# Two edits to a planner's inputs in a hybrid encoder layer: where the embedding gate's last four row blocks are cast, and where the last feed-forward part's first two units begin

## Chip, cores and metric

The kernel runs on one core of one Trainium2 chip. The metric is device time in microseconds (us) of one execution. Before the change three timed runs gave 1155.58, 1153.28 and 1151.23 us, so a median of 1153.28 us. One more execution was profiled.

## What is computed

One encoder layer on 256 rows of width 2048, in float32. Cut to the matrix products, which are nearly all of the work:

```python
u = rms_norm(h, g_mix_pre) @ w_in                       # 2048 x 5120
mixed = concat(norm(attention), norm(recurrence)) @ w_out
h = h + rms_norm(mixed, g_mix_post)
fn = rms_norm(h, g_ffn_pre)
ff = (silu(fn @ w_ffn_gate) * (fn @ w_ffn_up)) @ w_ffn_down   # inner width 5632
h = h + rms_norm(ff, g_ffn_post)
gate = sigmoid(rms_norm(h, g_ple_pre) @ w_ple_gate)     # 2048 x 2048
h = h + rms_norm(gate * (p @ w_ple_proj), g_ple_post)
```

## The kernel before

**Products and weight tiles.** A product of two float32 matrices is made of three matmuls (`mm3`, lines 694 to 696, 705 to 707): each operand is split into a rounded part (`hi`, `wh`) and the rest (`lo`, `wl`), and hi*hi, lo*hi and hi*lo are summed in PSUM. A weight tile is 2 blocks of 128 rows by 512 columns, 512 KB. It goes through three engines: SyncE (SP) issues its load into a raw buffer `wr` (line 568, or 551 in the feed-forward stage), ScalarE (ACT) rounds it into `wh` (line 643, `hi_stream`), VectorE (DVE) subtracts to get `wl` (line 656, `lo_stream`), and TensorE (PE) then runs 12 matmuls of 128x512 on it (`products`): 2 blocks, 2 halves of the 256 rows, 3 matmuls each. The third matmul of each three reads `wl`, so it can start later than the first two. There are four pairs `wh`/`wl` (`W_BUFS`) and four buffers `wr` (`R_BUFS`): a cast must wait until PE is done with the tile four back, and a load until DVE is done with the tile four back. Some loads of the feed-forward stage use further buffers, named `third` and `lower` in the trace.

**The order of the work.** Each engine gets its instructions in one fixed order. That order comes from a planner (`Plan`, lines 93 to 212) that runs when the kernel is built: every helper is a generator that yields the engine and estimated cost of its next instruction, and the planner takes the one that could start first, by its estimated clocks plus a bias (`late`). `plan.add(gen, ready, late)` hands it a generator that is not to start before `ready`. The order of PE's main products is written out by hand (`segs`); everything else is fitted around it.

**The feed-forward stage** runs in three parts (`PARTS`) of 4, 4 and 3 column chunks of the inner width. Each part makes its chunks (gate and up products, line 1890 on, group kind "up"), moves them into transposed form and multiplies them by `w_ffn_down` (kind "down"). Most groups save products in the manner of Strassen's scheme: some pairs of row blocks are treated as a unit of 2x2 blocks that needs seven products instead of eight. Such a unit begins with `four_products` (line 718), four of the seven, which need two weight tiles of which one is a sum of weight blocks: DVE makes the sums at lines 591, 595 and 601 (`sum_stream`) from a tile in `wr` or `third` and one in `lower`. The table `FOURS` (line 522) tells at which pair of weight tiles of the group ahead each unit of the next group begins. The last part's first down group has two units; its entry, ("up3", "down2"), is (2, 4): the first unit begins ahead of the third pair of the last up group, the second ahead of the fifth and last pair.

**The embedding gate.** Its left operand is the normed residual stream, transposed: 16 row blocks of 128 (`hP`, in the trace `hT_ffn_hi` and `hT_ffn_lo`). `next_norm` makes the new `h` on DVE in four chunks of 512 columns. Three of them are transposed by PE (line 330). The last goes through `turn_h` (line 1590): DVE transposes 32x32 squares (line 1596), 16 DMAs of 32 KB move the squares into the tile `mT` (`moved`, line 349, 12 of them issued by POOL and 4 by SP), and then four times ACT makes a block of `hT_ffn_hi` (line 317) and DVE a block of `hT_ffn_lo` (line 319). These are row blocks 12 to 15. The gate's products run over eight pairs of row blocks and, in turns, over the first two column chunks: tiles 0 and 1 use blocks 0 and 1, and so on, so that tiles 12 and 13 use blocks 12 and 13 and tiles 14 and 15 use blocks 14 and 15. Below, "tile n" is the n-th weight tile of the embedding gate, counted from 0.

Of the kernel before, what the change touches and what calls it, by code (L numbers as in the profile page):

```python
# [72 lines left out]
LATE = 0.8  # L73
EARLY = 3
SOON = 2.0
ADDED = 6.0
AHEAD = 5
ISSUE = 160
# [148 lines left out]
def dve(n, take=None, give=None):  # L227
    return ("dve", COST["dve"] + 0.00104 * n, None, take, give)
# [11 lines left out]
def layer(ctx: ExitStack, tc: tile.TileContext, a: dict, out: bass.AP):  # L240
# [5 lines left out]
    plan = Plan(wr=R_BUFS, w=W_BUFS, sm=SM_BUFS, acc=4, ev=1, mid=2, bt=2, m2=1, mt=1, sq=1, T0=1, T1=1, T4=1, **{f"{s}{j}": n for s, m, n in (("p", 5, 1), ("t", 4, 0)) for j in range(m)}, wr0=1, w0=1)  # L246
# [52 lines left out]
    def col(name, i):  # L299
        c = VEC_COLS[name][0] + i  # L300
        return vec[:, c : c + 1]
# [13 lines left out]
    def gained_split(hi, lo, src, g, give=None):  # L315
        yield act(S)
        nc.scalar.activation(hi, src, AF.Copy, scale=g)  # L317
        yield dve(S, give=give)
        nc.vector.scalar_tensor_tensor(  # L319
            out=lo, in0=src, scalar=g, in1=f32(hi), op0=ALU.mult, op1=ALU.subtract  # L320
        )
# [11 lines left out]
    def moved(e, here, take, tile_of, turn=True, pool=()):  # L333


        if turn:
            flat = e.rearrange("p t n -> p (t n)")
            yield dve(2 * N)
            nc.vector.transpose(out=flat, in_=flat)
        src = e.rearrange("p t (k j b) -> p t k j b", j=4, b=32)  # L340
        mT = None
        for j in range(4):
            for i in range(4):
                first = None if mT else take
                yield ("pool" if i in pool else "dma", COST["move"], None, first, None)
                if mT is None:
                    mT = tile_of()
                dst = mT.rearrange("p t k (i b) -> p t k i b", b=32)
                (nc.gpsimd if i in pool else nc.sync).dma_start(  # L349
                    dst[32 * j : 32 * j + 32, :, :, i, :],  # L350
                    src[32 * i : 32 * i + 32, :, :, j, :],
                )
        done(here)
        return mT.rearrange("p t k q -> p k t q")
# [16 lines left out]
    def done(event):  # L371
        event.t = plan.now
# [63 lines left out]
    class Group:  # L436
# [84 lines left out]
    }  # L521
    FOURS = {
        ("up0", "up3"): (3, 5, 7), ("up3", "up3"): (2, 3, 4), ("up3", "down4"): (2, 3, 3, 4),
        ("down4", "down4"): (1, 2, 3, 3), ("down4", "up3"): (1, 2, 3), ("up3", "down2"): (2, 4),
    }
    fours = {}

# [82 lines left out]
    def added(dst, src, ev):  # L610
        yield ("pool", COST["move"], None, None, None)
        nc.gpsimd.dma_start(dst, src, accum_op=ALU.add)  # L612
        plan.now += ADDED
        done(ev)

    def last_sum(i):
        late, last, j, js, _, _ = fours[i]
        b = OUT[j]
        there = Event()
        yield from added(blocks()[:, b, :], late[:, 0, :], there)  # L620
        yield there
        if j == js[-1]:
            raws[last] = blocks()[:, slice(3, 7, 3) if not js[0] else slice(1, 8, 6) if js[1:] else slice(7, 8), :]
            done(ev_raw[last, 2])
# [21 lines left out]
    def lo_stream():  # L646
        last_one = max(f[1] for f in fours.values())
        for i in range(len(tiles)):
# [16 lines left out]
            if i in fours:  # L665
                plan.add(last_sum(i), plan.now, -2 * SOON)

# [50 lines left out]
    def four_products(group, j, i):  # L718
# [16 lines left out]
        if last:  # L735
            plan.add(made_of_four(group), plan.clk["pe"] + plan.SEM, -SOON)
            plan.run()

    def made_of_four(group):

        (C1, _, _), (C2, _, _) = group.chunks
        (q1, q7), (q5, q6) = C1.accs, C2.accs
        there = Event()

        def second():
            yield act(N)
            nc.scalar.copy(q7, v)
            done(there)

        yield ev_rf  # L750
        yield act(N)
        u, v = (t2["pool"].tile([P, N], F32, tag="junk", name="u", bufs=2) for _ in range(2))
        nc.scalar.copy(u, q1)
        yield dve(N)
        nc.vector.tensor_tensor(out=u, in0=u, in1=q6, op=ALU.subtract)
        yield dve(N)
        nc.vector.tensor_tensor(out=v, in0=u, in1=q7, op=ALU.subtract)
        plan.add(second(), plan.now, -SOON)
        yield dve(N)
        nc.vector.tensor_tensor(out=q6, in0=q5, in1=v, op=ALU.subtract)  # L760
        yield dve(N)
        nc.vector.tensor_tensor(out=q5, in0=q5, in1=u, op=ALU.subtract)
        yield there
        done(group.made)
# [768 lines left out]
    def next_norm(sub, nxt, rstd, ev_rstd, g_next):  # L1533
# [24 lines left out]
        for c in range(4):  # L1558
            if c > 1:
                yield nxt.ev[4 * c - 8]  # L1560
            for b in range(2):
                sl = slice(c * N + b * S, c * N + (b + 1) * S)
                for t in range(NT):
                    yield dve(S)
                    nc.vector.scalar_tensor_tensor(
                        out=h[:, t, sl], in0=mg[:, t, sl], scalar=ro[:, t : t + 1],
                        in1=h[:, t, sl], op0=ALU.mult, op1=ALU.add,
                    )
                if c < TURNED:
                    plan.add(transpose_h(4 * c + 2 * b, hi, lo, nxt, sub.gname), plan.now)  # L1570
            if c >= TURNED:
                plan.add(turn_h(c, hi, lo, nxt, sub.gname), plan.now, -SOON)
        yield nxt.ev[4 * TURNED - 3]
# [16 lines left out]
    def turn_h(c, hi, lo, nxt, gname):  # L1590

        for t in range(NT):
            yield dve(N, take=None if t else "mid")
            if not t:
                e = mid_tile()
            nc.vector.transpose(out=e[:, t, :], in_=t2["h"][:, t, c * N : (c + 1) * N])
        there = Event()
        mT = yield from moved(e, there, "mt", mT_tile, turn=False, pool=(0, 1, 2) if nxt is hP else ())
        plan.free["mid"].append(plan.now)
        yield there  # L1600
        for b in range(4):
            kk = 4 * c + b
            yield from gained_split(
                *(x[:, kk, :].rearrange("p (t q) -> p t q", t=NT) for x in (hi, lo)), mT[:, b],
                col(gname, kk), give="mt" if b == 3 else None,
            )
            done(nxt.ev[kk])
# [106 lines left out]
    hP = Act()  # L1714
# [3 lines left out]
    def gate_post(f):  # L1718
        def post(ch):
            yield ev_rf  # L1720
            for t in range(NT):
                yield act(N, SILU, take=None if t else "mid")
                if t == 0:
                    es[f] = mid_tile()
                nc.scalar.activation(
                    es[f][:, t, :], ch.accs[t], AF.Silu, scale=rstd_f[:, t : t + 1]
                )
            ch.release()
        return post

    def mid_tile():
        return t2["pool"].tile([P, NT, N], F32, tag="mid", name="mid", bufs=2)
# [4 lines left out]
    def up_post(f, mid, kk0, g, soon):  # L1737

        def post(ch):
            yield g.free  # L1740
            e = es.pop(f)
            for t in range(NT):
                yield dve(N)
                nc.vector.scalar_tensor_tensor(
                    out=e[:, t, :], in0=ch.accs[t], scalar=rstd_f[:, t : t + 1], in1=e[:, t, :],
                    op0=ALU.mult, op1=ALU.mult,
                )
            ch.release()
            there = Event()
            mT = yield from moved(e, there, "mt", mT_tile, pool=(0, 2) if soon else range(4))  # L1750
            plan.free["mid"].append(plan.now)
            yield there
            plan.add(carried(mid, kk0, mT), plan.now + (0.5 if soon else {0: 12.0, 9: 6.0}.get(f, 3.0)), -SOON if soon else 0.0)
        return post

    def carried(mid, kk0, mT):
        summed = any(kk0 <= kx < kk0 + 4 for kx in mid.ev_sums)
        for b in range(0, 4, 2):
            kk = kk0 + b
            i, j = divmod(kk, 8)  # L1760
            hi, lo = mid.tiles(i)
            yield from split(
                *(by_tile(x[:, j : j + 2, :]) for x in (hi, lo)), mT[:, b : b + 2], 2 * S,
                give="mt" if b and not summed else None,
            )
            mid.pair(kk)
        if summed:
            plan.add(mid_sums(mid, kk0, mT), plan.now + (20.0 if mid.name[-1] == str(2) else 0.0))
# [106 lines left out]
    for part, (f0, f1) in enumerate(PARTS):  # L1875
        mid = Mid(f"mid{part}")
        last_part = part == len(PARTS) - 1
        for f in range(f0, f1):
            slot = ring()
            g = Chunk(gate_post(f), slot=slot)  # L1880
            u = Chunk(up_post(f, mid, (f - f0) * 4, g, f == f1 - 1), late=(-3 if f == f1 - 1 else -1) * SOON, slot=slot)
            groups.append(Group(
# [331 lines left out]
```

## Time and profile before

| what | value |
|---|---|
| median of the three timed runs | 1153.28 us |
| the profiled execution, its own time | 1154.53 us |
| span of its trace, first to last instruction | 1152.7 us |
| TensorE busy | 1139.3 us (99%) |
| VectorE busy | 923.4 us (80%) |
| ScalarE busy | 722.0 us (63%) |
| mean granted TensorE clock | 0.996 |

The page of the profile gives busy times and the chain of work that ended last. A row of the timeline gives the start and the length of an instruction, and in square brackets how long its engine sat idle before it and what ended that. Matmuls overlap, so that the distance between two starts, not the length, tells how fast PE goes.

### The profile page before, as it was taken

The page shows a single profiled execution, that of the slowest core. Times are in us where ns is not written, and L with a number is a line of the kernel's source. Part 1 is how long each engine was busy: PE and PEld are TensorE (multiplying, and loading weights), DVE is VectorE, ACT ScalarE, POOL GpSimd, SP SyncE. Part 2 cuts the span into 40 slices and gives each one's busy share as a digit, 9 for nine tenths or more (in the row PEclk, how much of TensorE's full clock was granted, in tenths as well). Part 3 has the DMA queues.
Part 4 walks back from the last instruction along what each step waited for, and adds up shares of the span by engine and source line. Part 5 has one row for each costly group of instructions (what it writes and reads, how often), then busy time and mean ns, then how long its engine had stood idle before and what let it go on. Part 6 is the DMA issues. An engine that isn't in the chain of part 4 may idle for free.

```text
span 1152.7 us, 15162 instructions
## 1 busy us (share of the span) xinstructions
PE 1139.3 (99%) x5199; PEld 946.3 (82%) x5199; DVE 923.4 (80%) x1161; ACT 722.0 (63%) x954; POOL 145.7 (13%) x232
## 2 busy tenths in 40 slices
PE   9999999999999999999999999999999999999897
PEld 7888888888888888888888888888888888888786
DVE  6578786888468779998988898989988888769474
ACT  7777777876447645656566556666555655557473
POOL 0000000000000033142110223312111303101000
PEclk9999999999999999999999999999999999999999
DMA  9867665546685996787877786897887678866661
GB/s 323 287 188 224 186 180 191 178 150 207 226 287 176 316 291 210 239 243 218 282 259 221 248 239 213 252 273 238 259 303 247 200 246 271 287 237 213 200 216 73
DMA packets 110270, 267.97 MB, mean 232 GB/s; under 512 B 36272, under 2 KB 43184, under 8 KB 108784
## 3 DMA queue, kind: packets, MB, share of 16 engines
q1 hardware_dynamic: 96304, 243.17, 62.2%
q0 software_dynamic: 13456, 23.48, 10.3%
q8 instruction: 40, 0.66, 0.2%
q10 hardware_dynamic: 432, 0.35, 0.1%
q14 instruction: 38, 0.31, 0.1%
HBM read 249.12 MB, written 9.44 MB: 224 GB/s over the span
## 4 chain that ended last, share of the span: by engine, by line
PE 94%; ACT 2%; DVE 2%; DMA 1%; SPq 0%; issue 0%; ACTq 0%
PE acc L696 24%; PE acc L695 24%; PE acc L694 24%; PE acc L707 6%; PE acc L706 6%; PE acc L705 6%; PE tr L330 1%; ACT wh L643 1%; DVE wl L656 1%; DMA wr<-in_w_ple_gate 1%; DMA sq<-ev 0%; ACT junk L1579 0%; DMA wr<-in_w_in 0%; PE pg L362 0%; PE pg L361 0%
## 5 line engine op out<-in xcount | busy, mean ns | idle before, releaser
L656 DVE TENSOR_TENSOR wl<-wr,wh 128x1024 fp32r<-128x1024 f32 (+1 forms) x304 | 363.1, 1208 | 107.9 <-ACT wh L643 106.5
L643 ACT CAST wh<-wr 128x1024 fp32r<-128x1024 f32 (+1 forms) x304 | 314.9, 1043 | 183.8 <-PE acc L695 133.3
L349 POOL DMA_DIRECT2D mT<-mid x164 | 96.3, 600 | 625.6 <-ACT wh L643 482.3
L695 PE MATMUL acc<-wh,hT_mix_lo 128*128 128x512 f32 x420 | 163.6, 390 | 0.3 <-DVE hT_mix_lo L319 0.3
L694 PE MATMUL acc<-wh,hT_mix_hi 128*128 128x512 f32 x420 | 163.7, 390 | 0.0
L696 PE MATMUL acc<-wl,hT_mix_hi 128*128 128x512 f32 x420 | 163.4, 389 | 0.0
L696 PE MATMUL acc<-wl,hT_hi 128*128 128x512 f32 x320 | 124.5, 390 | 0.0
L694 PE MATMUL acc<-wh,hT_hi 128*128 128x512 f32 x316 | 124.4, 394 | 0.0
L695 PE MATMUL acc<-wh,hT_lo 128*128 128x512 f32 x316 | 123.1, 390 | 0.0
L643 ACT CAST wh<-ple 128x1024 fp32r<-128x1024 f32 (+1 forms) x65 | 64.9, 1005 | 75.8 <-DVE ple L595 44.6
L695 PEld LDWEIGHTS acc<-wh,hT_mix_lo 128*128 128x128 f32 x420 | 78.8, 188 | 17.2 <-DVE hT_mix_lo L319 1.0
L696 PEld LDWEIGHTS acc<-wl,hT_mix_hi 128*128 128x128 f32 x420 | 78.8, 188 | 16.4
L694 PEld LDWEIGHTS acc<-wh,hT_mix_hi 128*128 128x128 f32 x420 | 78.8, 188 | 16.3
L656 DVE TENSOR_TENSOR wl<-ple,wh 128x1024 fp32r<-128x1024 f32 (+1 forms) x65 | 75.2, 1160 | 7.6 <-ACT wh L643 7.4
L696 PEld LDWEIGHTS acc<-wl,hT_hi 128*128 128x128 f32 x320 | 60.1, 188 | 12.9
L695 PEld LDWEIGHTS acc<-wh,hT_lo 128*128 128x128 f32 x316 | 59.4, 188 | 11.5
L694 PEld LDWEIGHTS acc<-wh,hT_hi 128*128 128x128 f32 x316 | 59.4, 188 | 11.4
L696 PE MATMUL acc<-wl,hT_ffn_hi 128*128 128x512 f32 x104 | 41.4, 398 | 3.5 <-DVE wl L656 3.5
L612 POOL DMA_DIRECT2D ple<-in_w_ffn_up x27 | 24.1, 893 | 161.6 <-DVE wl L656 121.3
L694 PE MATMUL acc<-wh,hT_ffn_hi 128*128 128x512 f32 x104 | 41.5, 399 | 0.3 <-ACT hT_ffn_hi L317 0.3
L695 PE MATMUL acc<-wh,hT_ffn_lo 128*128 128x512 f32 x104 | 41.1, 395 | 0.0
L643 ACT CAST wh<-third 128x1024 fp32r<-128x1024 f32 x30 | 31.5, 1051 | 11.3 <-PE acc L695 5.7
(439 smaller groups left out, 2441.8 us busy)
## 6 DMA issues: line engine op xcount, KB each, us to landing
wr<-in_w_in SPq DMA_DIRECT2D x77, 512.0 KB, 4.5
wr<-in_w_ffn_gate SPq DMA_DIRECT2D x74, 512.0 KB, 5.2
wr<-in_w_ffn_down SPq DMA_DIRECT2D x58, 512.0 KB, 5.7
wr<-in_w_ffn_up SPq DMA_DIRECT2D x51, 512.0 KB, 5.0
wr<-in_w_out SPq DMA_DIRECT2D x32, 512.0 KB, 4.0
wr<-in_w_ple_gate SPq DMA_DIRECT2D x32, 512.0 KB, 4.5
lower<-in_w_ffn_up SPq DMA_DIRECT2D x20, 512.0 KB, 6.3
lower<-in_w_ffn_down SPq DMA_DIRECT2D x16, 512.0 KB, 5.9
```

The source lines that it names most:

```text
L330: nc.tensor.transpose(tr[:, b, t * P : (t + 1) * P], e[:, t, sl], ident)
L349: (nc.gpsimd if i in pool else nc.sync).dma_start(dst[32 * j : 32 * j + 32, :, :, i, :], src[32 * i : 32 * i + 32, :, :, j, :],)
L612: nc.gpsimd.dma_start(dst, src, accum_op=ALU.add)
L643: nc.scalar.copy(his[i][:, 0 : src.shape[1], :] if n == 2 else his[i][:, j, :], src)
L656: nc.vector.tensor_tensor(out=los[i][:, m, :], in0=src, in1=f32(his[i][:, m, :]), op=ALU.subtract)
L694: nc.tensor.matmul(accs[t], hi[:, sl], his[i][:, j, :], start=st, stop=False, **group)
L695: nc.tensor.matmul(accs[t], lo[:, sl], his[i][:, j, :], start=False, stop=False, **group)
L696: nc.tensor.matmul(accs[t], hi[:, sl], los[i][:, j, :], start=False, stop=sp, **group)
L705: nc.tensor.matmul(dst, x[0], wh, start=start, stop=False, skip_group_check=seeded)
L706: nc.tensor.matmul(dst, x[1], wh, start=False, stop=False, skip_group_check=seeded)
L707: nc.tensor.matmul(dst, x[0], wl, start=False, stop=stop, skip_group_check=seeded)
```

## The change

It has two parts.

1. The four casts and subtractions of row blocks 12 to 15 become a generator of their own, `split_turned`. `turn_h` hands it to the planner once the moves of `mT` are written, for the embedding gate not before 6.0 us of planned time later (`LATER`); for the feed-forward stage the delay is 0 and the order there is as before.
2. The entry ("up3", "down2") of `FOURS` becomes (4, 4): both units begin ahead of the last pair.

```diff
+LATER = 6.0
...
-        ("down4", "down4"): (1, 2, 3, 3), ("down4", "up3"): (1, 2, 3), ("up3", "down2"): (2, 4),
+        ("down4", "down4"): (1, 2, 3, 3), ("down4", "up3"): (1, 2, 3), ("up3", "down2"): (4, 4),
...
         yield there
+        plan.add(split_turned(c, mT, hi, lo, nxt, gname), plan.now + (LATER if nxt is hP else 0.0), -SOON)
+
+    def split_turned(c, mT, hi, lo, nxt, gname):
         for b in range(4):
             kk = 4 * c + b
             yield from gained_split(
                 *(x[:, kk, :].rearrange("p (t q) -> p t q", t=NT) for x in (hi, lo)), mT[:, b],
                 col(gname, kk), give="mt" if b == 3 else None,
             )
             done(nxt.ev[kk])
```

What the planner makes of it is seen in the order of the instructions on each engine. The lines of the changed kernel are shifted by 1, and by 4 from `split_turned` on (line 317 becomes 318, 643 becomes 644, 656 becomes 657, 591 becomes 592).

On ACT, in the embedding gate, before the change: `wr_9043` is the raw tile 8, `wr_9061` tile 9, `wr_9079` tile 10, `wr_9100` tile 11, `wr_9141` tile 12.

```order
L643 CAST wh_9122<-wr_9043 128x1024
L643 CAST wh_9131<-wr_9061 128x1024
L317 ACTIVATE hT_ffn_hi_8873<-mT_9028,vec_69 128x256
L643 CAST wh_9145<-wr_9079 128x1024
L317 ACTIVATE hT_ffn_hi_8873<-mT_9028,vec_69 128x256 x2
L643 CAST wh_9165<-wr_9100 128x1024
L317 ACTIVATE hT_ffn_hi_8873<-mT_9028,vec_69 128x256
L643 CAST wh_9187<-wr_9141 128x1024
```

The same place after the change:

```order
L644 CAST wh_9122<-wr_9043 128x1024
L644 CAST wh_9131<-wr_9061 128x1024
L644 CAST wh_9143<-wr_9079 128x1024
L644 CAST wh_9164<-wr_9100 128x1024
L318 ACTIVATE hT_ffn_hi_8872<-mT_9028,vec_69 128x256 x2
L644 CAST wh_9191<-wr_9141 128x1024
L318 ACTIVATE hT_ffn_hi_8872<-mT_9028,vec_69 128x256
L644 CAST wh_9203<-wr_9153 128x1024
L318 ACTIVATE hT_ffn_hi_8872<-mT_9028,vec_69 128x256
```

The casts of tiles 10 and 11 now stand ahead of the first cast that needs `mT`.

On DVE, at the same place, before the change:

```order
L656 TENSOR_TENSOR wl_9123<-wr_9043,wh_9122 128x1024
L319 SCALAR_TENSOR_TENSOR hT_ffn_lo_8874<-mT_9028,vec_69,hT_ffn_hi_8873 128x256 x3
L656 TENSOR_TENSOR wl_9132<-wr_9061,wh_9131 128x1024
L319 SCALAR_TENSOR_TENSOR hT_ffn_lo_8874<-mT_9028,vec_69,hT_ffn_hi_8873 128x256
L656 TENSOR_TENSOR wl_9146<-wr_9079,wh_9145 128x1024
```

And after it:

```order
L657 TENSOR_TENSOR wl_9123<-wr_9043,wh_9122 128x1024
L657 TENSOR_TENSOR wl_9132<-wr_9061,wh_9131 128x1024
L657 TENSOR_TENSOR wl_9144<-wr_9079,wh_9143 128x1024
L657 TENSOR_TENSOR wl_9165<-wr_9100,wh_9164 128x1024
L320 SCALAR_TENSOR_TENSOR hT_ffn_lo_8873<-mT_9028,vec_69,hT_ffn_hi_8872 128x256 x2
L657 TENSOR_TENSOR wl_9192<-wr_9141,wh_9191 128x1024
```

Before, the `wl` of tile 9 stood behind three subtractions that need `mT`; now those of tiles 9, 10 and 11 stand ahead of all of them.

On DVE, at the last up group, after the change. `third` in its first row holds a gate tile (third pair) and later, as `wr_8138` does for the first unit, a tile of the second unit; `lower` holds the other tile of each unit in turn; `ple` holds the sums.

```order
L657 TENSOR_TENSOR wl_8153<-third_2887,wh_8152 128x1024
L657 TENSOR_TENSOR wl_8174<-wr_8024,wh_8173 128x1024
L657 TENSOR_TENSOR wl_8188<-wr_8054,wh_8187 128x1024
L592 TENSOR_TENSOR ple_2886<-wr_8138 128x512
L596 TENSOR_TENSOR ple_2886<-ple_2886,lower_4017 128x512
L602 TENSOR_TENSOR wr_8138<-wr_8138,lower_4017 128x512
L657 TENSOR_TENSOR wl_8211<-wr_8115,wh_8210 128x1024
L657 TENSOR_TENSOR wl_8230<-ple_2886,wh_8229 128x1024
L592 TENSOR_TENSOR ple_2886<-third_2887 128x512
L596 TENSOR_TENSOR ple_2886<-ple_2886,lower_4017 128x512
L602 TENSOR_TENSOR third_2887<-third_2887,lower_4017 128x512
L657 TENSOR_TENSOR wl_8252<-wr_8138,wh_8251 128x1024
```

Before, the first unit's sums and both its `wl` stood ahead of the third pair. Now the first unit's second `wl` (the last row) stands behind the second unit's three sums. On PE the four weight tiles of the third and fourth pair, 48 matmuls, stand ahead of the first unit's 12 instead of behind them.

## The prediction

> **What bounds the kernel now.** I read the page first, then who PE waits for, then the table by stage, then the timelines where PE stands still.
>
> ```profile
> span 1152.7 us, 15162 instructions
> PE 1139.3 (99%) x5199; PEld 946.3 (82%) x5199; DVE 923.4 (80%) x1161; ACT 722.0 (63%) x954; POOL 145.7 (13%) x232
> PE 94%; ACT 2%; DVE 2%; DMA 1%; SPq 0%; issue 0%; ACTq 0%
> PE acc L696 <- DVE wl L656: 3.5, 1, 3.5
> PE final L2056 <- ACT diag L2054: 2.0, 1, 2.0
> PE warm L2123 <- POOL ones L295: 1.1, 1, 1.1
> ```
>
> PE sets the time: 99% busy, 94% of the chain. A change that leaves the number of matmuls as it is can win only what PE loses. Its waits (line, released by, total, times, longest) hold one of 3.5 us inside the program; the next two are at the end and at the start, where nothing is edited. The table by stage (us, then busy us of PE, PEld, DVE, ACT, POOL, then the granted clock, DMA share, GB/s) says where:
>
> ```profile
> 960.00:980.00 20.00, 20.00 (x90) 16.57 (x89) 15.01 (x16) 11.12 (x13) 4.82 (x7) 1.00 0.94 327
> 1075.00:1085.00 10.00, 6.54 (x22) 4.95 (x21) 7.12 (x9) 5.59 (x8) 0.00 (x0) 0.83 0.44 137
> ```
>
> The first stage is where the units of `FOURS` are moved: PE busy 20.00 of 20.00 us, so nothing can be won there, and DMA at 0.94, so something can be lost. The second is where the embedding gate's blocks are cast: PE busy 6.54 of 10, clock 0.83. PE, ACT and DVE there, in order of time:
>
> ```profile
> 1075.25 0.39 PE L695 MATMUL acc<-wh,hT_ffn_lo 128*128 128x512 f32 x1
> 1079.10 0.77 PE L696 MATMUL acc<-wl,hT_ffn_hi 128*128 128x512 f32 x1 [3.46 <-DVE wl L656]
> 1079.67 0.63 PE L694 MATMUL acc<-wh,hT_ffn_hi 128*128 128x512 f32 x1
> 1080.10 0.63 PE L695 MATMUL acc<-wh,hT_ffn_lo 128*128 128x512 f32 x1
> ...
> 1084.00 0.39 PE L695 MATMUL acc<-wh,hT_ffn_lo 128*128 128x512 f32 x1
> ...
> 1092.39 0.39 PE L696 MATMUL acc<-wl,hT_ffn_hi 128*128 128x512 f32 x1
> 1068.78 1.05 ACT L643 CAST wh<-wr 128x1024 fp32r<-128x1024 f32 x1 [1.54 <-DMA wr<-in_w_ple_gate]
> 1075.13 0.51 ACT L317 ACTIVATE hT_ffn_hi<-mT,vec 128x256 fp32r<-128x256 f32 x1 [5.30 <-DMA wr<-in_w_ple_gate]
> 1067.28 1.23 DVE L656 TENSOR_TENSOR wl<-wr,wh 128x1024 fp32r<-128x1024 f32 x1 [0.77 <-ACT wh L643]
> 1075.68 0.48 DVE L319 SCALAR_TENSOR_TENSOR hT_ffn_lo<-mT,vec,hT_ffn_hi 128x256 fp32r<-128x256 f32 x1 [7.18 <-ACT hT_ffn_hi L317]
> 1077.83 1.22 DVE L656 TENSOR_TENSOR wl<-wr,wh 128x1024 fp32r<-128x1024 f32 x1
> ```
>
> PE has run the first two matmuls of tile 9 and waits for its `wl`. ACT made the `wh` of tile 9 from 1068.78 to 1069.83. But the `wl` stands on DVE behind three subtractions that need `mT`, so it begins only at 1077.83, after DVE has sat idle for 7.18 us. ACT stands too, 5.30 us, ahead of its first cast out of `mT`. The row puts that wait down to a weight load. By the program, that cast waits for `mT`'s moves alone, which use some of the same counters; the POOL rows below agree. **The blocks that hold both queues up, 12 to 15, are not wanted by PE before tile 12.**
>
> **Part one: what it removes.** 37 matmuls lie from 1084.00 to 1092.39, so full speed is 0.2268 us from one start to the next. The matmul at 1084.00 is the 15th after the one at 1075.25 and at full speed would start at 1075.25 + 15 x 0.2268 = 1078.65. The stop costs 1084.00 - 1078.65 = **5.35 us**. Of these, 1079.10 - 1075.25 - 0.23 = 3.62 are standing still, and 1.73 are the slow matmuls behind it (1079.67 to 1080.10: 0.43 apart).
>
> The slow matmuls are a rule of the Trainium skill, "TensorE: Matmul & The Clock Gate", section "Part 1: The HAM clock gate": after an idle window of about 3.4 us PE falls to half its clock, and needs as long a busy one to come back. The trace agrees (3.46 us idle, then 0.43 against 0.227 us, for 3.5 us). By that rule a remainder of 1 or 2 us would cost only its own length; by the one row here, scaled, it would cost half as much again. The sum needs neither if the stop goes whole.
>
> Does it? I follow the new order with the loads as they landed. These are the last moves of `mT` on POOL, and the loads of tiles 10, 11 and 12 with the us from issue to landing:
>
> ```profile
> 1067.63 1.16 POOL L349 DMA_DIRECT2D mT<-mid  x2 [0.56 <-issue]
> mT<-mid POOLq DMA_DIRECT2D x2, 32.0 KB, 6.7
> 1063.87 0.33 SPq L568 DMA_DIRECT2D wr<-in_w_ple_gate  x1
> wr<-in_w_ple_gate SPq DMA_DIRECT2D x1, 512.0 KB, 6.8
> 1065.01 0.33 SPq L568 DMA_DIRECT2D wr<-in_w_ple_gate  x1
> wr<-in_w_ple_gate SPq DMA_DIRECT2D x1, 512.0 KB, 9.1
> 1068.53 0.33 SPq L568 DMA_DIRECT2D wr<-in_w_ple_gate  x1
> wr<-in_w_ple_gate SPq DMA_DIRECT2D x1, 512.0 KB, 7.2
> ```
>
> - The last moves land 6.7 us after 1067.6 to 1068.2, about 1074.9, which is where ACT went on (1075.13).
> - Tile 9: cast to 1069.83, `wl` next on DVE, done by 1071.1. PE wants it at 1075.5.
> - Tile 10: landed 1063.87 + 6.8 = 1070.7, cast to 1071.7, `wl` 1072.9. PE wants it one tile later, 12 x 0.2268 = 2.72, at 1078.2. Its buffer `wh` comes free when tile 6 is done: tile 9 began at 1075.0, two tiles of 2.72 earlier is 1069.6.
> - Tile 11: landed 1074.1, cast to 1075.2, `wl` 1076.4; wanted 1080.9.
> - Then two casts out of `mT`, to 1076.1, the cast of tile 12 (landed 1075.7) to 1077.2, its `wl` 1078.4; PE reaches tile 12 at 1083.2 and wants the `wl` at 1083.6.
>
> Every step has over 4 us to spare, and nothing new stands still long enough to matter: that ACT still waits for tile 11 until 1074.1 is idle time which it had before. The four casts and subtractions are the same; they move, and none is added. Moving two raw buffers' release forward also moves the loads of tiles 13 and 14 forward, from about 1079 to 1071 and 1073, beside the last moves; a load took 6.8 to 9.1 us here, so both land by 1083, and are wanted from 1085.9. On SP the reload of `ple` goes behind one load and the gain of the last norm; both are read only when the first two column chunks are done, behind tile 15. **Part one: -5.35 us**, bounds -3.6 (the slow matmuls stay, for some other reason) and -5.4 (no more than the stop is there).
>
> **Part two.** The same 60 matmuls in another order, no instruction more, PE busy throughout. So it wins nothing, and costs what arrives late. Before, the two ends of this stage:
>
> ```profile
> 961.13 0.39 PE L705 MATMUL acc<-wh,sums 128*128 128x512 f32 x1
> 974.73 0.39 PE L705 MATMUL acc<-wh,sums 128*128 128x512 f32 x1
> third<-in_w_ffn_down SPq DMA_DIRECT2D x1, 512.0 KB, 7.1
> lower<-in_w_ffn_down SPq DMA_DIRECT2D x1, 512.0 KB, 9.1
> 960.64 0.33 SPq L1448 DMA_DIRECT2D gain_g_ffn_post<-in_g_ffn_post  x1
> 961.16 0.33 SPq L551 DMA_DIRECT2D third<-in_w_ffn_down  x1
> 961.54 0.42 SPq L551 DMA_DIRECT2D lower<-in_w_ffn_down  x1
> 959.92 1.22 DVE L656 TENSOR_TENSOR wl<-third,wh 128x1024 fp32r<-128x1024 f32 x1
> 970.71 0.69 DVE L595 TENSOR_TENSOR ple<-ple,lower 128x512 f32<-128x512 f32 x1 [1.72 <-DMA lower<-in_w_ffn_down]
> 971.58 0.62 ACT L311 CAST mid2h<-mT 128x512 fp32r<-128x512 f32 x1 [6.70 <-DMA mT<-mid]
> 974.65 1.23 DVE L656 TENSOR_TENSOR wl<-third,wh 128x1024 fp32r<-128x1024 f32 x1 [0.24 <-ACT wh L643]
> ```
>
> The first unit ran from 961.13 and the second from 974.73. After, the third and fourth pair (48 x 0.2268 = 10.9) run from 961.13, the first unit at 972.0, the second at 974.7, as before. The second unit's loads decided DVE's clock: `lower` landed 961.54 + 9.1 = 970.7, and the second `wl` of that unit began at 974.65, ended at 975.9, with PE wanting it two products later, at 974.73 + 8 x 0.2268 = 976.5. That is 0.7 us to spare **before**.
>
> After, DVE has the second unit's three sums ahead of the first unit's second `wl`, which PE wants at 972.0 + 8 x 0.2268 = 973.8. By the 0.61 us that a sum takes DVE, from the sum that waits for `lower` to the end of that `wl` are 0.61 + 0.61 + 1.2 = 2.4 us, so `lower` must land by 971.4. `third` and `lower` are issued when the `wl` out of `third` ends: before at 961.1, now no later, since three sums and a `wl` fewer stand ahead of it on DVE (about 960). And the 1 MB gain, which stood ahead of them on SP at 960.64, is now behind. So `lower` lands between 969.4 and 970.7 with its 9.1 us: 0.7 to 2 us to spare. The second unit's second `wl` waits for two casts out of the earlier `mT`, which ACT began at 971.58: 971.58 + 2 x 0.62, the unit's cast 1.05 and its `wl` 1.2 give 975.1, some 0.5 more with DVE's two subtractions of 0.69 ahead of it: 0.9 us to spare. **Part two: 0**, bounds 0 and about +3 (1 to 2 us of delay in a stage where loads took 7 to 9 us, with 0.7 to 2 us to spare, and half as much again for the clock). I take 0: every margin comes out no smaller than the 0.7 us that was enough before.
>
> **The sum** against the profiled execution: span 1152.7 - 5.35 = 1147.4, own time 1154.53 - 5.35 = 1149.2. That execution is 1.25 us above the median of the runs, so the forecast is 1153.28 - 5.35 = **1147.9 us**, 0.46% less.
>
> **The rivals.**
> - *Part two gives some back.* `lower`, or the earlier `mT`, lands 2 to 3 us later than reckoned, and PE stops at 972 to 976. For it: DMA at 0.94, margins of 0.7 to 2 us. Against: the gain is out of the way. Time: 1149.5 to 1152.
> - *The stop moves to tile 12.* From the landing of `mT`, two casts, tile 12's cast and `wl` take 3.3 us, so PE waits if `mT` lands after 1083.6 - 3.3 = 1080.3, against 1074.9 to 1075.1 before. What could delay it: the loads of tiles 13 and 14, now beside its last moves. With `mT` at 1083 PE would stop for 2.7 us: 1150.6 to 1152. The Trainium skill, "DMA: Bandwidth & Descriptors", section "Queues, rings and completion order", has each DMA engine take packets from its queues in turn, which speaks for such a delay and against the change; the row here (6.7 us for 32 KB, with three loads in flight) shows that it is already so. 5.2 us of cover stand against it.
> - *The change doesn't reach the stop.* If tile 9's `wl` waited for something of its own, the order would not matter: 1153.3. Against: its `wh` was ready 8 us before DVE came to it.
> - *Slower.* In part two, at 972: the second unit's sums hold up DVE, and with it all later `wl`, if `lower` comes late. Every us past 971.4 is a us of PE, and it decides from 971.4 + 5.35 = 976.8 on; it passes the bound for slower (5.8 us more) at 982.5, a landing of 22 us against 9.1. Time: 1159 and up. Only a queue on DMA that no row shows would do it.
>
> **How the numbers follow.** Chances: forecast 0.74, part two gives back 0.13, tile 12 0.05, not reached 0.04, slower 0.04. The forecast's own range is 1146.4 to 1149.4: the three runs lie 4.35 us apart, a median of them varies by perhaps a third of that either way. The range reaches up over the give-back to 1151.5, and down to 1146.0 (the stop may have been longer in the runs than in the profiled execution, which I cannot see): together about 0.85. Half a per cent, about what a measurement of this kernel can tell from no change, is 5.77 us, and the line lies at 1147.5, 0.4 us below the forecast. So faster by more than that gets a little under half of the forecast's 0.74, 0.35; within it 0.61; slower 0.04.
>
> **What would show it right or wrong.** Right: no PE wait on L657's `wl` in the embedding gate, the clock there 1.00 instead of 0.83, ACT's first cast out of `mT` behind the casts of tiles 10 and 11, a span near 1147.4, and PE still full from 960 to 980. Wrong: a PE stop at tile 12, a stop at the first or second unit, or a landing of the last `mT` move after 1080. If PE's waits are gone and the time is not, the cause is outside both places and my reading of the stop as whole on the path is wrong.

## The result, and the profile after

The changed kernel takes 1147.91 us (median of six runs, 1147.71 to 1148.57) against 1153.59 (1151.23 to 1155.58): a ratio of 0.9951, with a 95% interval of 0.9938 to 0.9964. Its profiled execution took 1148.01 us.

The page of the changed kernel, its head and its first row:

```profile
span 1146.2 us, 15164 instructions
PE 1137.3 (99%) x5199; PEld 945.7 (83%) x5199; DVE 923.8 (81%) x1161; ACT 723.1 (63%) x954; POOL 145.5 (13%) x232
```

For whom PE waits after the change (total, times, longest):

```profile
PE final L2060 <- ACT diag L2058: 2.0, 1, 2.0
PE warm L2127 <- POOL ones L296: 1.1, 1, 1.1
PE acc L696 <- DVE hT_mix_lo L320: 0.3, 1, 0.3
PE acc L695 <- ACT hT_ffn_hi L318: 0.3, 1, 0.3
```

The wait of 3.5 us for `wl` is gone, and none came in its place. The two stages, by the table:

```profile
960.00:980.00 20.00, 20.00 (x90) 16.53 (x89) 17.13 (x21) 12.84 (x16) 4.64 (x7) 1.00 1.04 338
1075.00:1085.00 10.00, 10.00 (x46) 8.29 (x45) 6.49 (x8) 5.67 (x9) 0.00 (x0) 1.00 0.80 251
```

PE is full in both, and the clock of the second is 1.00 where it was 0.83. The timelines of ACT, DVE and PE around tile 9 after the change:

```profile
1068.78 1.05 ACT L644 CAST wh<-wr 128x1024 fp32r<-128x1024 f32 x1 [1.60 <-DMA wr<-in_w_ple_gate]
1070.86 1.05 ACT L644 CAST wh<-wr 128x1024 fp32r<-128x1024 f32 x1 [1.02 <-DMA wr<-in_w_ple_gate]
1072.53 1.05 ACT L644 CAST wh<-wr 128x1024 fp32r<-128x1024 f32 x1 [0.63 <-DMA wr<-in_w_ple_gate]
1074.74 0.91 ACT L318 ACTIVATE hT_ffn_hi<-mT,vec 128x256 fp32r<-128x256 f32 x2 [1.15 <-DMA wr<-in_w_ple_gate]
1069.87 1.22 DVE L657 TENSOR_TENSOR wl<-wr,wh 128x1024 fp32r<-128x1024 f32 x1 [1.43 <-ACT wh L644]
1071.94 1.23 DVE L657 TENSOR_TENSOR wl<-wr,wh 128x1024 fp32r<-128x1024 f32 x1 [0.85 <-ACT wh L644]
1073.62 1.22 DVE L657 TENSOR_TENSOR wl<-wr,wh 128x1024 fp32r<-128x1024 f32 x1 [0.45 <-ACT wh L644]
1075.28 0.89 DVE L320 SCALAR_TENSOR_TENSOR hT_ffn_lo<-mT,vec,hT_ffn_hi 128x256 fp32r<-128x256 f32 x2 [0.44 <-ACT hT_ffn_hi L318]
1074.17 0.39 PE L696 MATMUL acc<-wh,hT_ffn_lo 128*128 128x512 f32 x1
1074.39 0.39 PE L697 MATMUL acc<-wl,hT_ffn_hi 128*128 128x512 f32 x1
```

The second matmul of tile 9 starts at 1074.17, and the third, 0.22 us later, not 3.85. Its `wl` was done at 1071.1; those of tiles 10 and 11 at 1073.2 and 1074.8, before DVE begins its first subtraction out of `mT` at 1075.28. The wait for `mT` is still there, but nothing that PE wants soon stands behind it.

The spans differ by 6.5 us. Compared matmul by matmul, PE is 1.08 us further on than before at the second matmul of tile 9, and 6.42 us further on when the slow matmuls of the profile of before are over: 5.34 us are won at the stop. The 1.08 us come from far ahead of both edits, nearly all from one short wait in the profiled execution of before, which is not in that of any other kernel here:

```profile
188.69 0.55 PE L330 MATMUL tr<-ident,ev 128*128 128x128 f32 x3 [0.91 <-ACT ev L1024]
```

So the second matmul of tile 9 stood at 1075.25 before and stands at 1074.17 now. Times read from these two profiles must be shifted by 1.08 us to be compared, and that is not a gain of the change.

### The profile page after: what moved, and what is told of

Same layout as the page of the kernel before. It is cut to its first block, busy times and chain, and to the rows that moved or that the text cites. A ratio compares the mean times of both kernels' runs of the same rounds, so it can differ in the third digit from the quotient of the medians.

```text
span 1146.2 us, 15164 instructions
## 1 busy us (share of the span) xinstructions
PE 1137.3 (99%) x5199; PEld 945.7 (83%) x5199; DVE 923.8 (81%) x1161; ACT 723.1 (63%) x954; POOL 145.5 (13%) x232
## 4 chain that ended last, share of the span: by engine, by line
PE 95%; ACT 1%; DMA 1%; DVE 1%; SPq 0%; issue 0%; ACTq 0%; DVEq 0%
PE acc L696 24%; PE acc L697 24%; PE acc L695 24%; PE acc L707 6%; PE acc L706 6%; PE acc L708 6%; PE tr L331 1%; DMA sq<-ev 1%; ACT wh L644 1%; DMA wr<-in_w_in 0%; PE pg L362 0%; PE pg L363 0%; PE pg L361 0%; DVE wl L657 0%; DMA av<-in_w_rg_i 0%
```

## The experiments

The theory: PE lost 5.35 us because DVE's `wl` of tile 9 stood behind subtractions that need `mT`; part one takes that away, and part two is worth nothing. Rivals: the units' place brings a part; ACT's standing still, not DVE's, is what stops PE; the price of a stop is its length alone.

| kernel | median us (range) | ratio to before (95%) |
|---|---|---|
| changed kernel | 1147.91 (1147.71 to 1148.57) | 0.9951 (0.9938 to 0.9964) |
| part one alone | 1148.07 (1147.53 to 1148.46) | 0.9951 (0.9939 to 0.9964) |
| part two alone | 1154.1 (1151.55 to 1155.82) | 1.0002 (0.9993 to 1.0012) |
| subtractions alone | 1149.39 (1148.87 to 1151.43) | 0.9966 (0.9953 to 0.9978) |
| LATER = 2.0 | 1148.3 (1147.23 to 1148.52) | 0.9948 (0.9933 to 0.9963) |
| LATER = 12.0 | 1147.67 (1147.4 to 1148.63) | 0.9947 (0.9933 to 0.9961) |
| LATER = 20.0 | 1151.57 (1150.19 to 1152.77) | 0.9983 (0.9974 to 0.9992) |
| before, stop filled | 1152.0 (1151.09 to 1153.99) | 0.9986 (0.9977 to 0.9995) |

The kernel before ran at 1153.59 us (1151.23 to 1155.58) beside the changed kernel, at 1153.48 (1151.48 to 1155.74) beside the two parts alone, the subtractions alone and LATER = 20.0, and at 1153.77 (1152.87 to 1155.76) beside the other three.

### Part one alone

```diff
-        ("down4", "down4"): (1, 2, 3, 3), ("down4", "up3"): (1, 2, 3), ("up3", "down2"): (4, 4),
+        ("down4", "down4"): (1, 2, 3, 3), ("down4", "up3"): (1, 2, 3), ("up3", "down2"): (2, 4),
```

> Part one alone: split_turned with its 6.0 us stays, the entry of FOURS goes back to (2, 4). Theory (the whole gain is the stop of PE at tile 9, 5.35 us, and the units' new place is worth nothing): no wait of PE in the embedding gate, ratio to before 0.995, about 1147.9 us. Rival (the units' new place brings a part of it): 1149 to 1152, and a wait or slow matmuls between 960 and 1003 us.

Measured 1148.07 us, a span of 1146.3 us, and no wait of PE in the embedding gate beyond the 0.3 us that every kernel has. The whole gain comes with part one.

### Part two alone

```diff
-        ("down4", "down4"): (1, 2, 3, 3), ("down4", "up3"): (1, 2, 3), ("up3", "down2"): (2, 4),
+        ("down4", "down4"): (1, 2, 3, 3), ("down4", "up3"): (1, 2, 3), ("up3", "down2"): (4, 4),
```

> Part two alone: the kernel before with the entry of FOURS at (4, 4). Theory: the stop at tile 9 stands as before (3 to 4 us of waiting and some 8 matmuls 0.43 us apart), ratio 1.000, about 1153.3 us, within 1 us of the kernel before. Rival (the units' place counts): 1150 to 1152, or above 1155 if a load comes late there.

Measured 1154.1 us, ratio 1.0002. PE's wait, and ACT and DVE at tile 9, in this kernel:

```profile
PE acc L696 <- DVE wl L656: 3.8, 1, 3.8
1074.16 0.51 ACT L317 ACTIVATE hT_ffn_hi<-mT,vec 128x256 fp32r<-128x256 f32 x1 [3.92 <-DMA mT<-mid]
1076.85 1.22 DVE L656 TENSOR_TENSOR wl<-wr,wh 128x1024 fp32r<-128x1024 f32 x1
```

The stop stands as before. Here the profile names the moves of `mT` as what ACT waited for, where the profile of before named a weight load; this bears out the reading by the program.

### The subtractions alone

The units as before. On DVE the four subtractions come behind the `wl` of tiles 9 to 12. On ACT all four casts out of `mT` stand ahead of the casts of tiles 10 to 13 (before, one stood ahead of tile 10's and three ahead of tile 11's).

```diff
...
+            yield act(S)
+            nc.scalar.activation(views[0], mT[:, b], AF.Copy, scale=col(gname, kk))
+            plan.add(low_turned(kk, b, mT, *views, nxt, gname), plan.now + LATER, -SOON)
```

> The units at (2, 4) as before; on ACT the four casts out of mT are ahead of the casts of tiles 10 and 11 as they were before, and only the four subtractions on DVE come 6.0 us of planned time later, behind the wl of tiles 9 to 12. Theory (the stop was DVE's queue: the wl of tile 9 behind subtractions that need mT): PE gets tile 9 in time; the wl of tile 10 waits for four casts out of mT, from about 1074.9: 4 x 0.41 + 1.05 + 1.2 = 1078.8 where PE wants it at 1078.2, so a wait of 0.5 to 0.8 us without slow matmuls, about 1148.5 us. Rival (ACT standing before mT is what stops PE): a stop nearly as long as before, 1152 to 1153.

Measured 1149.39 us: 1.3 above part one alone, 4.1 below before. PE's waits, ACT, DVE and PE in this kernel:

```profile
PE acc L697 <- DVE wl L657: 0.5, 1, 0.5
PE acc L695 <- ACT wh L644: 0.3, 1, 0.3
1074.01 1.71 ACT L1613 ACTIVATE hT_ffn_hi<-mT,vec 128x256 fp32r<-128x256 f32 x4 [6.09 <-DMA wr<-in_w_ple_gate]
1075.62 3.88 ACT L644 CAST wh<-wr 128x1024 fp32r<-128x1024 f32 x4
1076.68 3.50 DVE L657 TENSOR_TENSOR wl<-wr,wh 128x1024 fp32r<-128x1024 f32 x3 [7.51 <-ACT wh L644]
1077.96 0.50 PE L697 MATMUL acc<-wl,hT_ffn_hi 128*128 128x512 f32 x1 [0.53 <-DVE wl L657]
1078.30 0.39 PE L695 MATMUL acc<-wh,hT_ffn_hi 128*128 128x512 f32 x1
```

ACT stands still for 6.09 us, longer than before, and DVE for 7.51, yet PE is idle for only 0.34 + 0.53 us, at tile 10 and no longer at tile 9. Counted from start to start PE loses 1.4 us, against 5.35 before. So most of the stop was DVE's order. My 0.5 to 0.8 us missed the shorter wait for `wh` itself. One of the five runs took 1151.43 us at a mean clock of 0.996, the others 0.997 to 0.999; the clock may have fallen in it, but it has no trace.

The last 1.4 us are not ACT's share of the stop before. My expectation says that ACT's casts stand as they did there, and that is wrong: three more casts out of `mT`, 0.4 us each, stand ahead of tile 10's. An estimate from this trace, with one cast out of `mT` ahead as before: tile 10's `wh` is there at 1075.5 and its `wl` at 1076.7, and PE wants them at 1076.2 and 1076.65, so it would wait for 0.1 us. By this estimate DVE's order made nearly the whole stop; no run here has exactly that order.

### Later still: 2.0, 12.0 and 20.0

```diff
-LATER = 6.0
+LATER = 2.0
```

and the same with 12.0 and 20.0.

> The changed kernel with LATER = 2.0: on ACT only the cast of tile 10 stands ahead of the four casts out of mT (6.0 puts tiles 10 and 11 there), on DVE the wl of tiles 9 and 10 ahead of the four subtractions. Theory: what counts is that the wl of tiles 9 and 10 don't wait for mT; tile 11's wl ends near 1077.8 on the clock of the changed kernel, and PE wants it at about 1079.8, so no wait and 1147.9 us. Rival (the longer way is needed): a wait at tile 11, 1148.5 to 1150.

> The changed kernel with LATER = 12.0: the casts of tiles 10 to 14 stand ahead of the casts out of mT. Tile 14 is cast when PE leaves tile 10, one tile sooner than tile 15 in the run with 20.0: the casts out of mT come 2.72 us sooner than there, where PE waited 1.3 and 0.7 us. Theory: row block 12 is there 0.6 us before PE reaches tile 12, so no wait, 1147.9 us, or a few tenths more if the subtractions come just late. Rival (every cast put ahead costs): 1149 to 1150.

> The changed kernel with LATER = 20.0: the casts of tiles 10 to 15 all stand ahead of the first cast out of mT, and the wl of tile 15 ahead of the subtractions. Theory (a cast must wait until PE is done with the tile four back): tile 15 is cast only when PE leaves tile 11, at about 1083.2 on the clock of the profile before, so that row block 12 comes at 1084.8 (hi) and 1085.9 (lo): PE waits 1.5 and then about 1 us at tile 12, 2.5 to 3 us in all. If so short a wait costs only its own length, about 1150.5 us; if every us of waiting costs one and a half as in the stop before, about 1152. Rival (PE has slack there): no wait, 1147.9.

With 2.0 and 12.0 the time is that of the changed kernel, and PE has no wait in the embedding gate. With 2.0 the `wl` of tiles 11 to 14 come one after the other, the first from 1078.02. It is done at 1079.2, later than the expected 1077.8, and PE wants it at 1080.1, so 0.9 us are to spare:

```profile
1078.02 4.62 DVE L657 TENSOR_TENSOR wl<-wr,wh 128x1024 fp32r<-128x1024 f32 x4
```

With 12.0 the casts out of `mT` come at 1079.56, the subtractions at 1080.84, and PE wants the first of each at 1081.36 and 1081.59. They are done 1.3 and 0.3 us before that:

```profile
1079.56 1.71 ACT L318 ACTIVATE hT_ffn_hi<-mT,vec 128x256 fp32r<-128x256 f32 x4
1080.84 1.67 DVE L320 SCALAR_TENSOR_TENSOR hT_ffn_lo<-mT,vec,hT_ffn_hi 128x256 fp32r<-128x256 f32 x4
```

With 20.0 tile 15's cast has to wait for PE to leave tile 11, and what tile 12 needs stands behind it. ACT and PE there:

```profile
1081.41 1.04 ACT L644 CAST wh<-wr 128x1024 fp32r<-128x1024 f32 x1 [1.67 <-PE acc L696]
1082.36 1.70 ACT L318 ACTIVATE hT_ffn_hi<-mT,vec 128x256 fp32r<-128x256 f32 x4
1082.92 0.50 PE L695 MATMUL acc<-wh,hT_ffn_hi 128*128 128x512 f32 x1 [1.32 <-ACT hT_ffn_hi L318]
1084.16 0.80 PE L696 MATMUL acc<-wh,hT_ffn_lo 128*128 128x512 f32 x1 [0.74 <-DVE hT_ffn_lo L320]
1084.76 0.63 PE L697 MATMUL acc<-wl,hT_ffn_hi 128*128 128x512 f32 x1
1085.18 0.63 PE L695 MATMUL acc<-wh,hT_ffn_hi 128*128 128x512 f32 x1
...
1087.64 0.40 PE L695 MATMUL acc<-wh,hT_ffn_hi 128*128 128x512 f32 x1
```

This is a stop at tile 12, the second rival of the prediction. PE is idle for 1.32 and 0.74 us, which from start to start are 1.48 + 1.01 = 2.5 us, as expected. The matmuls behind it are 0.42 us apart up to 1087.5 and cost 1.7 us more, as much as behind the longer stop before, although no idle piece was longer than 1.32 us. The median is 3.7 us above the changed kernel's. But four of the eleven runs took 1150.2 to 1150.6 us, hardly more than the waiting alone. Their mean clocks, 0.998 to 0.999 against 0.997 in the profiled execution, would fit that these four had no slow matmuls; they have no trace to show it.

### Before, with the stop filled

```diff
...
+                            fill = bank("fill").rearrange("p k s -> p (k s)")
+                            for _ in range(FILL):
+                                nc.tensor.matmul(fill, hi[:, sl], his[i][:, j, :], start=True, stop=True)
```

(`FILL` is 12, between the second and the third matmul of tile 9.)

> The kernel before, with 12 extra matmuls of 128x512 on tile 9's own operands into an unused PSUM bank, between the second and the third matmul of tile 9; nothing reads them, and all other orders are as before. They fill 12 x 0.2268 = 2.7 of the 3.6 us in which PE stands still, so that it is idle for under 1 us. Theory (the stop costs 3.6 us of waiting in every run, and on top a slow clock that differs from run to run, which is why runs of the kernel before lie 4 us apart and those of the changed one 1): no matmul 0.43 us apart behind the stop, clock 0.998 in nearly all runs, 1147.9 + 3.6 = 1151.5 us, runs within 1.5 us. Rival (the runs differ because the moves of mT land at different times, and the slow matmuls are a fixed 1.7 us): the same spread of 4 us, and a median at 1151.8 or above.

Measured 1152.0 us, against 1153.77 of the kernel before beside it: 1.8 us less with 12 matmuls more. PE at tile 9, and the stage in the table:

```profile
1074.39 2.88 PE L704 MATMUL fill<-wh,hT_ffn_hi 128*128 128x512 f32 x12
1077.82 0.50 PE L705 MATMUL acc<-wl,hT_ffn_hi 128*128 128x512 f32 x1 [0.54 <-DVE wl L657]
1078.15 0.39 PE L697 MATMUL acc<-wh,hT_ffn_hi 128*128 128x512 f32 x1
1075.00:1085.00 10.00, 9.46 (x43) 7.47 (x42) 7.22 (x9) 5.50 (x8) 0.00 (x0) 1.00 0.55 168
```

PE has useless work instead of standing still, the clock stays at 1.00, and the time falls by 1.8 us (0.6 to 2.7 by the interval), where the prediction had put the slow matmuls at 1.73. From start to start PE still loses 3.6 us between the second and the third matmul of tile 9. The mean clock was 0.997 to 0.999 in all eleven runs, where the kernel before had 0.995 to 0.997 beside it. One half of my theory fell: the runs lie 2.9 us apart, from 1151.09 to 1153.99, not under 1.5, and those of the kernel before beside it lie 2.9 us apart too. So filling the stop took nothing off the spread, and in these runs none of it can be put down to the slow matmuls; here the rival was nearer. That `mT` lands at different times would fit, but these runs leave no trace to show it, and the cause of the spread stays open.

## Why the prediction was right, point by point

- **What bounds the kernel, and where it loses.** Right. PE's wait at tile 9 is gone from the profile after, and with it the stage's clock of 0.83.
- **Part one, 5.35 us.** Right in mechanism and size: 1153.59 - 1147.91 = 5.7 us between the medians, which 5.35 agrees with inside the interval, and 5.34 us at the stop itself, matmul by matmul. Its two terms were measured apart. The slow matmuls, put at 1.73 us, are the 1.8 us by which the filled kernel gains. The standing still, put at 3.62, is what the filled kernel keeps: 3.6 us at tile 9 in its trace, and 1152.0 - 1147.9 = 4.1 us between medians, with the runs 2.9 us apart. That the median of 1147.91 falls on the forecast of 1147.9 is partly luck, since the runs before lie over 4 us apart.
- **That both queues hold up PE.** Both did stand still, but the prediction did not say how the stop divides. With DVE's order alone mended, PE lost 1.4 us instead of 5.35, and by the estimate above these 1.4 come from ACT's order in that kernel, not from the one before. So DVE's queue made the stop.
- **The new order tile by tile.** Right. With the shift of 1.08 us taken off, the forecasts were 1071.8 for tile 10's `wl`, 1075.3 for tile 11's and 1074.1 for the first cast out of `mT`; they were done, or begun, at 1073.2, 1074.8 and 1074.74. The largest miss, 1.4 us at tile 10, did not use up the margin there.
- **Part two, 0.** Right, and shown alone: 1.0002. The margins were larger than I gave them. In the changed kernel SP issues the second unit's `lower`, DVE adds it, and DVE makes the second `wl` of each unit, and PE reads those, at:

```profile
957.32 0.43 SPq L552 DMA_DIRECT2D lower<-in_w_ffn_down  x1
965.74 0.69 DVE L596 TENSOR_TENSOR ple<-ple,lower 128x512 f32<-128x512 f32 x1
966.95 1.22 DVE L657 TENSOR_TENSOR wl<-wr,wh 128x1024 fp32r<-128x1024 f32 x1
972.14 1.23 DVE L657 TENSOR_TENSOR wl<-third,wh 128x1024 fp32r<-128x1024 f32 x1 [0.18 <-ACT wh L644]
972.75 0.39 PE L708 MATMUL acc<-wl,mid2h 128*128 128x512 f32 x1
975.47 0.39 PE L708 MATMUL acc<-wl,mid2h 128*128 128x512 f32 x1
```

  The loads were issued at 957, where the prediction, less the shift, had 958.9. The first unit's second `wl` is done at 968.2 and wanted at 972.75, 4.6 us to spare where I gave 0.7 to 2; the second unit's at 973.4 for 975.47, 2.1 where I gave 0.9. The `wl` out of `third`, which lets both loads go, was done at 956.9, two us sooner than I took it to be. The direction was right; the size of the margins was not.
- **The price of a short stop.** The prediction set the page "TensorE: Matmul & The Clock Gate" of the Trainium skill, section "Part 1: The HAM clock gate", by which a wait well under 3.4 us costs its own length, against the one row, scaled, by which it costs half as much again. The runs show neither as it stands. In the profiled execution with LATER = 20.0 waits of 2.5 us were followed by 1.7 us of slow matmuls, the same as behind the 3.62 us before, so that this price is not in proportion to the wait. The times of the runs near 1150.4 look as if they paid none of it, as the page has it. The sum needed neither, since the stop went whole.
- **The half per cent.** 0.49% was measured, 0.46% forecast. The interval, 0.36% to 0.62%, leaves open on which side of a half per cent the gain lies, as the prediction's chances did.

None of the rivals took place in the changed kernel. None of the other kernels is clearly better than it: all those without the stop lie between 1147.7 and 1148.3 us.

## What to carry to other kernels

When an engine serves two streams in one queue, look at what stands behind an instruction whose input is late, not at that instruction: `mT` was as late after the change as before, and cost nothing. Ask for each late input how many tiles of the urgent stream fit ahead of it; here one was enough (LATER = 2.0), five did no harm (12.0) but left only 0.3 us, and the sixth (20.0) turned the order round, because its own buffer came free only when PE, which was to be kept from waiting, had done the tile four back. And before taking two edits as one, run each alone: one of these two did all of it.

## What the runs showed of the hardware that was not expected

The half rate comes in pieces of one length. In the traces' record of the granted clock it lasts 3.413 us behind the stop in the kernel before (1079.15 to 1082.56), in part two alone and with LATER = 20.0, and so costs about half of that, 1.7 us, whether PE had stood still for 3.6 or for 2.5 us. Each of these pieces begins a whole number of times 3.413 us (315, 314 and 316) after the clock first reached full speed, and that moment lay anywhere from 4.0 to 7.2 us after the first instruction in the nine profiles.

In the 3.413 us just ahead of these pieces PE had been idle for 3.36, 3.02 and 1.99 us, the last in two parts. With the stop filled and with the subtractions alone no such stretch held more than 0.54 us of idling there, and the clock stayed full. That one and the same stop costs 1.7 us in one run and nothing in another because it falls differently on these stretches would fit the runs with LATER = 20.0, but is not shown. And 12 useless matmuls in a stop of 3.6 us made the whole kernel 1.8 us quicker.
